# Head norms whose row transfers go by GpSimd's queue, in a hybrid attention, retention and pooling encoder

## The chip, the core and the metric

The kernel runs on one core of a Trainium2 chip. Five engines work side by side, each through its own instructions in a fixed order: TensorE (PE; its weight loads are shown as PEld), VectorE (DVE), ScalarE (ACT), GpSimd (POOL) and SyncE (SP), which here issues transfers. The metric is the device time of one execution in microseconds (us); lower is better.

## The reference

Two layers over a sequence of 512 tokens with 1024 features, then a final RMSNorm. Each layer normalises its input, projects it, gives the columns to three groups of heads, multiplies each group by its own SiLU gate and maps the three back with one output projection. The change concerns the norms at the end of the heads of groups A and B:

```python
# A: differential attention, 4 heads, values of 128 columns
o = rmsnorm(o, subln_w) * (1.0 - lam_init)
o_a = o.reshape(B_, S_, A_V_COLS) * jax.nn.silu(ag)
# B: bidirectional retention, 4 heads, values of 128 columns
o = o * lax.rsqrt(jnp.mean(o * o, axis=-1, keepdims=True) + EPS)
o_b = o_b * jax.nn.silu(bg)
# C: multi-scale pooling; then
mixed = jnp.concatenate([o_a, o_b, o_c], axis=-1)
return x + jnp.einsum('bse,ed->bsd', mixed, w_out)
```

So each of 2 x 8 heads needs one number per token, the reciprocal root of the mean square over its 128 features.

## The kernel before

All matmuls are in fp32 split into a high and a low part, three products for each (`mm3`): one 128x512 product is three matmuls. Weights come from DRAM as 512 KB pieces into `wraw` (2 buffers), and ACT and DVE split each into `wh` and `wl` (5 buffers each). A projection (`proj_T`, `proj_tok`) adds up 24 matmuls in one of three PSUM banks called `pj`. A gate (`gate`) is such a projection, a tanh on ACT and one multiply on DVE; that multiply is the last reader of its `pj` bank and so frees it.

A head ends with a result of 128 features (partitions) by 512 tokens in the one PSUM bank `ov`, and `headnorm` follows:

- ACT copies `ov` into `hn`, tokens reordered; DVE multiplies `ov` by the gate into `og`. `hn` and `og` have one buffer each, so the next head's copy waits for this head's last multiply.
- PE transposes `hn` into `tp` (4 matmuls of 128 columns), ACT squares and sums each quarter into `st` (the tile `st4`), DVE adds EPS, and GpSimd raises to the power -0.5: 512 numbers, 128 partitions by 4.
- A transfer writes these to a DRAM tile `row` of 512 numbers (`row<-st`), and a second one reads the row back into all 128 partitions of `hn` (`hn<-row`, 256 KB). The second waits for the first to land. Both are issued by SP, whose queue also issues the weight pieces and the decay and bias tables (`wide`).
- DVE multiplies `og` by `hn`, called the last multiply below, and the head is split into `mB` or `mAC` for the output projection.

The pooling heads use `hn` too, with windows of `u` that GpSimd clears.

The order of the instructions is not written by hand. The program is recorded as operations with their dependences; `schedule` then plays it through with a duration for each operation from `cost` and a delay between engines from `LATENCY`, and always starts next, on the engine that is free first, the ready operation of the highest rank. The order that comes out is each engine's fixed order. A transfer on SP is counted by the lines below (times in ns): it ends 1100 plus its bytes at 360 per ns plus 908 after its start, later when others are under way.

```python
            if e == "SP":
                bus = max(bus, start + 1100) + op.time
                op.end = bus + 908
```

All instructions are emitted at one line (L1055 before, L1057 after), so the profile is read by the names of the tiles.

Of the kernel before, what the change touches and what calls it, by code (L numbers as in the profile page):

```python
# [15 lines left out]
P = 128  # L16
# [153 lines left out]
class Recorder:  # L170
# [9 lines left out]
    def add(self, name, engine, method, args, kw):  # L180
# [33 lines left out]
        for b in bases:  # L214
            b.left += 1
        op.bases, op.deps, op.users = bases, list(deps.values()), []
        op.time, op.hold = cost(engine, method, args, kw)
        self.ops.append(op)

# [103 lines left out]
def cost(engine, method, args, kw):  # L323

    out = args[0]
    n = out.idx.size if isinstance(out, View) else 0
    psum = any(isinstance(a, View) and a.base.space == "psum" for a in args)
    if engine == "PE":
        if method == "transpose":
            return 109, 109  # L330
        f32 = args[1].base.dt == F32 and not any(s[0] == "bitcast" for s in args[1].steps)
        if f32:
            return 2 * 110 + 4 * n * 0.417, 2 * 110 + 4 * n * 0.417
        t = max(107, n * 0.417) + 2.5
        return t, t
    if engine == "SP":
        nbytes = (out.p1 - out.p0) * n * 4 if isinstance(out, View) and out.base.space != "dram" else P * D * 4
        if isinstance(out, View) and out.base.space == "dram":
            nbytes = 16384
        return nbytes / 360.0, 475  # L340
    if engine == "DVE":
        if method == "tensor_tensor":
            t = 1.041 * n + 69
        elif method == "scalar_tensor_tensor":
            t = 1.041 * n + (130 if isinstance(args[2], View) else 69)
        elif method == "tensor_scalar":
            t = (1.17 if psum else 0.64) * n + 69
        elif method == "tensor_copy":
            t = (1.04 if psum else 0.521) * n + 68
        elif method == "reciprocal":  # L350
            t = 6.2 * n + 69
        elif method == "memset":
            t = 9
        else:
            t = 1.041 * max(n, 2) + 75
        return t, t
    if engine == "ACT":
        t = 0.833 * n + (52 if psum else 94)
        for k in ("bias", "scale"):
            t += 93 * isinstance(kw.get(k), View)  # L360
        t += 93 * ("accum_out" in kw)
        return t, t
    if method == "tensor_tensor" and kw["op"] == ALU.pow:
        return 300 + 164 * n, 300 + 164 * n
    if method == "tensor_tensor":
        return 60 + 2.2 * n, 60 + 2.2 * n
    return 60 + 1.3 * n, 60 + 1.3 * n


def record(ins: dict, out: bass.AP):  # L370
    nc = Recorder()
    x_d = ins["x"][0]

    def sb(tag, shape, bufs=1, dt=F32, name=None):
        return nc.tile("sb", tag, shape, bufs, dt)
# [102 lines left out]
    def transpose4(src):  # L478

        tp = tpp()  # L480
        for j in range(4):
            nc.tensor.transpose(tp[:, j * P:(j + 1) * P], src[:, j * P:(j + 1) * P], ident)
        return tp.rearrange("p (j c) -> p j c", j=4)
# [51 lines left out]
    def headnorm(ov, scale, g):  # L535

        o = sb("hn", [P, UW], 1)[:, 0:S]

        nc.scalar.copy(o.rearrange("p (j c) -> p j c", j=4), ov.rearrange("p (c j) -> p j c", j=4))
        og = sb("og", [P, S], 1)  # L540
        nc.vector.scalar_tensor_tensor(og, ov, scale, g, op0=ALU.mult, op1=ALU.mult)
        tv = transpose4(o)
        st = sb("st4", [P, 8], 2)
        for j in range(4):
            nc.scalar.activation(o[:, j * P:(j + 1) * P], tv[:, j, :], AF.Square, accum_out=st[:, j:j + 1])
        nc.vector.tensor_scalar(st[:, 0:4], st[:, 0:4], 1.0 / P, EPS, op0=ALU.mult, op1=ALU.add)
        nc.gpsimd.tensor_tensor(st[:, 4:8], st[:, 0:4], neghalf, op=ALU.pow)
        row = nc.tile("dram", "row", [S], 4, F32)
        nc.sync.dma_start(row.rearrange("(p j) -> p j", j=4), st[:, 4:8])
        rb = o  # L550
        nc.sync.dma_start(rb, row.partition_broadcast(P))
        nc.vector.tensor_tensor(og, og, rb, op=ALU.mult)
        return og

# [126 lines left out]
    class Layer:  # L681
# [155 lines left out]
        def b_head(self, h):  # L837
            dt_ = chunk_decay(4 * self.l + h)
            qk, qx, sx = self.qk["B", h // 2]
            hd = h % 2  # L840
            ov = ovp()
            for ch in range(2):
                cs = slice(256 * ch, 256 * ch + 256)
                lg = lgp()
                for j in range(2):
                    ms = slice((2 * ch + j) * P, (2 * ch + j + 1) * P)
                    js = slice(256 * j, 256 * j + 256)
                    nc.tensor.matmul(lg[:, js], qk[:, 2 + 2 * hd, ms], qk[:, hd, cs], start=True, stop=False)
                    nc.tensor.matmul(lg[:, js], qk[:, 3 + 2 * hd, ms], qk[:, hd, cs], start=False, stop=True)
                s = soft()  # L850
                nc.vector.scalar_tensor_tensor(s.rearrange("p (j c) -> p j c", j=2), lg.rearrange("p (j c) -> p j c", j=2), 0.125,
                                               dt_[:, :, ::-1], op0=ALU.mult, op1=ALU.mult)
                it = ttile([P, 2, S], F32R)
                split(it[:, 0, :], it[:, 1, :], s)
                for j in range(2):
                    m, js = 2 * ch + j, slice(256 * j, 256 * j + 256)
                    mm3(ov[:, cs], self.vh[:, m, h * P:(h + 1) * P], self.vl[:, m, h * P:(h + 1) * P],
                        it[:, 0, js], it[:, 1, js], j == 0, False)
                for x in range(2):
                    nc.tensor.matmul(ov[:, cs], sx[:, hd, x, 1 - ch, :], qx[:, hd, cs], start=False, stop=x == 1)  # L860
            self.to_mixed("B", h, headnorm(ov, 0.5, self.gates["bg", h]))
# [7 lines left out]
        def a_head(self, h):  # L869
            qk = self.qk["A", h]  # L870
            bt = toeplitz(gdram, h)
            ov = ovp()
            for half in range(2):
                ah, al = ttile([P, NT, 256], F32R), ttile([P, NT, 256], F32R)
                for i2 in range(2):
                    i = half * 2 + i2
                    st = sb("sm", [P, 8], 4)
                    e = []
                    for mp in range(2):
                        lg = lgp()  # L880
                        mm_stacked(lg, qk, mp, slice(i * P, (i + 1) * P))
                        s = soft()

                        nc.vector.tensor_tensor_reduce(s, lg, toep_tile(bt, i), scale=1.0, scalar=3e38,
                                                       op0=ALU.add, op1=ALU.min, accum_out=st[:, mp:mp + 1])
                        nc.scalar.activation(s, s, AF.Exp, bias=st[:, mp:mp + 1], scale=-1.0, accum_out=st[:, 4 + mp:5 + mp])
                        e.append(s)
                    nc.vector.reciprocal(st[:, 6:8], st[:, 4:6])
                    nc.vector.tensor_tensor(st[:, 7:8], st[:, 7:8], lam_t[self.l], op=ALU.mult)
                    nc.scalar.activation(e[1], e[1], AF.Copy, scale=st[:, 7:8])  # L890
                    nc.vector.scalar_tensor_tensor(e[0], e[0], st[:, 6:7], e[1], op0=ALU.mult, op1=ALU.subtract)
                    tv = transpose4(e[0])
                    split(ah[:, :, i2 * P:(i2 + 1) * P], al[:, :, i2 * P:(i2 + 1) * P], tv)
                for kt in range(NT):
                    mm3(ov[:, half * 256:(half + 1) * 256], self.vh[:, kt, h * P:(h + 1) * P],
                        self.vl[:, kt, h * P:(h + 1) * P], ah[:, kt, :], al[:, kt, :], kt == 0, kt == NT - 1)
            self.og[h] = headnorm(ov, cols[:, self.l:self.l + 1], self.gates["ag", h])
# [225 lines left out]
```

## Time and profile before

| | us |
|---|---|
| Median of 3 runs (670.14 to 670.65) | 670.25 |
| Profiled execution, its own time | 670.98 |
| Its span, first to last instruction | 669.2 |
| PE busy | 657.1 |
| DVE busy | 478.3 |
| ACT busy | 385.2 |
| POOL busy | 30.2 |

A busy PE is not yet a PE at its peak: matmuls overlap, and one of 512 columns shows some 0.4 us while the next starts about 0.23 us after it. A pause of PE is therefore read from the starts of two neighbours. In brackets behind an instruction stands how long its engine was idle before it and what ended that.

### The profile page before, as it was taken

The page shows a single profiled execution, that of the slowest core. Times are in us where ns is not written, and L with a number is a line of the kernel's source. Part 1 is how long each engine was busy: PE and PEld are TensorE (multiplying, and loading weights), DVE is VectorE, ACT ScalarE, POOL GpSimd, SP SyncE. Part 2 cuts the span into 40 slices and gives each one's busy share as a digit, 9 for nine tenths or more (in the row PEclk, how much of TensorE's full clock was granted, in tenths as well). Part 3 has the DMA queues.
Part 4 walks back from the last instruction along what each step waited for, and adds up shares of the span by engine and source line. Part 5 has one row for each costly group of instructions (what it writes and reads, how often), then busy time and mean ns, then how long its engine had stood idle before and what let it go on. Part 6 is the DMA issues. An engine that isn't in the chain of part 4 may idle for free. (4 is left out here: it accounts for less than half of the span.)

```text
span 669.2 us, 8859 instructions
## 1 busy us (share of the span) xinstructions
PE 657.1 (98%) x3173; PEld 538.0 (80%) x3173; DVE 478.3 (71%) x865; ACT 385.2 (58%) x735; POOL 30.2 (5%) x51
## 2 busy tenths in 40 slices
PE   8999999999999999999999999999999999999996
PEld 6887878887788888887888788778888878888885
DVE  5798886776788879875754878587558846887733
ACT  6646885534776776552524877244567756874321
POOL 0100000000000000001010000000100000000011
PEclk9999999999999999999999999999999999999999
DMA  8545454223234322244113414433331243212302
GB/s 309 202 153 165 116 153 111 95 97 103 66 102 122 116 80 63 91 114 123 64 64 111 141 64 96 121 121 84 80 111 59 69 134 109 92 63 81 110 31 95
DMA packets 29300, 71.59 MB, mean 107 GB/s; under 512 B 5460, under 2 KB 9716, under 8 KB 29256
## 3 DMA queue, kind: packets, MB, share of 16 engines
q1 hardware_dynamic: 29256, 71.02, 34.4%
q8 instruction: 25, 0.41, 0.3%
q14 instruction: 19, 0.16, 0.1%
HBM read 68.83 MB, written 2.18 MB: 106 GB/s over the span
## 5 line engine op out<-in xcount | busy, mean ns | idle before, releaser
L1055 PE MATMUL pj<-hh,wh 128*128 128x512 f32 x448 | 176.9, 398 | 2.1 <-DVE gate L1055 1.3
L1055 PE MATMUL pj<-hl,wh 128*128 128x512 f32 x448 | 176.4, 395 | 0.0
L1055 PE MATMUL pj<-hh,wl 128*128 128x512 f32 x448 | 176.0, 396 | 0.0
L1055 ACT CAST wh<-wraw 128x1024 fp32r<-128x1024 f32 (+1 forms) x97 | 100.8, 1039 | 84.3 <-PE pj L1055 65.5
L1055 DVE TENSOR_TENSOR wl<-wraw,wh 128x1024 fp32r<-128x1024 f32 (+1 forms) x97 | 117.3, 1209 | 35.0 <-ACT wh L1055 34.5
L1055 PEld LDWEIGHTS pj<-hh,wh 128*128 128x128 f32 x448 | 84.1, 188 | 21.8 <-DVE gate L1055 1.9
L1055 PEld LDWEIGHTS pj<-hh,wl 128*128 128x128 f32 x448 | 84.0, 188 | 18.3
L1055 PEld LDWEIGHTS pj<-hl,wh 128*128 128x128 f32 x448 | 84.2, 188 | 17.8
L1055 PE MATMUL pj<-wh,mAC 128*128 128x512 f32 (+1 forms) x264 | 86.8, 390 | 0.0
L1055 ACT ACTIVATE soft<-soft,sm 128x512 f32<-128x512 f32 x96 | 68.6, 721 | 21.8 <-DVE sm L1055 20.8
L1055 DVE TENSOR_TENSOR x<-x,pj 128x512 f32<-128x512 f32 (+1 forms) x65 | 43.8, 676 | 19.7 <-PE pj L1055 19.2
L1055 PEld LDWEIGHTS pj<-wh,mAC 128*128 128x128 f32 x264 | 48.8, 188 | 10.3 <-DVE mAC L1055 0.2
L1055 PE MATMUL pj<-wl,mAC 128*128 128x512 f32 (+1 forms) x132 | 51.5, 390 | 0.0
L1055 PE MATMUL lg<-qk 128*128 128x512 f32 (+1 forms) x192 | 50.3, 360 | 0.7 <-DVE soft L1055 0.4
L1055 DVE CUSTOM_DVE_ANT_0 soft<-lg,wide 128x512 f32<-128x512 f32 x64 | 43.1, 686 | 9.7 <-PE lg L1055 7.0
L1055 POOL TENSOR_TENSOR st<-st,neghalf 128x4 f32<-128x4 f32 (+1 forms) x28 | 25.0, 892 | 476.2 <-DVE st L1055 447.5
L1055 PE MATMUL pj<-wh,mB 128*128 128x512 f32 (+1 forms) x136 | 44.3, 382 | 0.0
L1055 PE MATMUL pj<-wh,hh 128*128 128x512 f32 x104 | 41.3, 397 | 0.4 <-DVE vl L1055 0.4
L1055 PE MATMUL pj<-wl,hh 128*128 128x512 f32 x104 | 41.4, 398 | 0.0
L1055 PE MATMUL pj<-wh,hl 128*128 128x512 f32 x104 | 41.1, 396 | 0.0
L1055 PEld LDWEIGHTS lg<-qk 128*128 128x128 f32 x192 | 32.5, 188 | 8.0 <-issue 1.5
L1055 PE MATMUL ov<-T,vh 128*128 128x256 f32 x192 | 38.8, 283 | 0.0
(156 smaller groups left out, 951.6 us busy)
## 6 DMA issues: line engine op xcount, KB each, us to landing
wraw<-in_wg SPq DMA_DIRECT2D x95, 512.0 KB, 3.3
hn<-row SPq DMA_DIRECT2D x16, 256.0 KB, 3.4
wide<-gd SPq DMA_DIRECT2D x8, 448.0 KB, 3.1
T<-in_xT_w SPq DMA_DIRECT2D x8, 258.0 KB, 4.9
x<-in_x SPq DMA_DIRECT2D x8, 256.0 KB, 5.2
wide<-dd SPq DMA_DIRECT2D x8, 256.0 KB, 5.1
out<-T SPq DMA_DIRECT2D x8, 256.0 KB, 2.1
qd<-dd SPq DMA_DIRECT2D x8, 128.0 KB, 4.5
```

The source lines that it names most:

```text
L1055: op.inst = getattr(getattr(tc.nc, name), method)(*[real(a) for a in op.args], **{k: real(v) for k, v in op.kw.items()})
```

## The change

`headnorm` issues its two transfers through GpSimd's queue in place of SP's, and `cost` gets a row for transfers on GpSimd: 2000 ns to the end of one that writes DRAM, 3800 ns of any other, and 600 ns for which GpSimd is held by it.

```diff
+    if engine == "POOL" and method == "dma_start":
+        return (2000 if out.base.space == "dram" else 3800), 600
     if engine == "SP":
...
         nc.gpsimd.tensor_tensor(st[:, 4:8], st[:, 0:4], neghalf, op=ALU.pow)
         row = nc.tile("dram", "row", [S], 4, F32)
-        nc.sync.dma_start(row.rearrange("(p j) -> p j", j=4), st[:, 4:8])
+        nc.gpsimd.dma_start(row.rearrange("(p j) -> p j", j=4), st[:, 4:8])
         rb = o
-        nc.sync.dma_start(rb, row.partition_broadcast(P))
+        nc.gpsimd.dma_start(rb, row.partition_broadcast(P))
         nc.vector.tensor_tensor(og, og, rb, op=ALU.mult)
```

SP's list loses 32 transfers (189 rows become 157) and is otherwise in the same order; GpSimd's gets them, each pair right behind its power. Since the planner now counts other times, its order changes on the other engines as well. On PE the two orders are the same up to row 816 of 2850, differ in places up to about row 1145 and again from about row 1805 to about row 2340, and are the same elsewhere but for one matmul near the end.

First place: DVE in the second layer, around the last multiply of the first retention head (`og_3768`) and the gate multiply that frees bank `pj_3652`. Before:

```order
L1055 TENSOR_TENSOR T_3859<-soft_3847,T_3859 128x512
L1055 TENSOR_TENSOR og_3768<-og_3768,hn_3742 128x512
L1055 TENSOR_TENSOR T_3867<-soft_3856,T_3867 128x512
L1055 TENSOR_TENSOR qx_3841<-soft_3582,qx_3841 64x512
L1055 TENSOR_TENSOR mB_3885<-og_3768,mB_3885 128x512
L1055 SCALAR_TENSOR_TENSOR soft_3897<-lg_3861,wide_3869 128x512
L1055 SCALAR_TENSOR_TENSOR soft_3904<-lg_3872,wide_3869 128x512
L1055 TENSOR_TENSOR wl_3911<-wraw_3772,wh_3899 128x1024
L1055 TENSOR_TENSOR T_3908<-soft_3897,T_3908 128x512
L1055 SCALAR_TENSOR_TENSOR gate_3852<-gate_3852,pj_3652 128x512
```

The same place in the changed kernel:

```order
L1057 TENSOR_TENSOR T_3859<-soft_3847,T_3859 128x512
L1057 TENSOR_TENSOR T_3867<-soft_3856,T_3867 128x512
L1057 TENSOR_TENSOR og_3768<-og_3768,hn_3742 128x512
L1057 TENSOR_TENSOR qx_3841<-soft_3582,qx_3841 64x512
L1057 SCALAR_TENSOR_TENSOR gate_3852<-gate_3852,pj_3652 128x512
L1057 TENSOR_TENSOR mB_3889<-og_3768,mB_3889 128x512
```

The last multiply stands one instruction later, and the gate multiply two behind it where it stood eight behind it.

Second place: PE where the next projection takes the bank that this gate multiply frees (`pj_0`: the number after the tile's name is the buffer here). Before:

```order
L1055 MATMUL pj_2_3648<-hh_0_3084,wl_3_3478 128x512
L1055 MATMUL pj_2_3648<-hh_0_3084,wh_1_3459 128x512
L1055 MATMUL pj_0_3931<-hh_0_3084,wh_0_3640 128x512
L1055 MATMUL pj_0_3931<-hl_0_3094,wh_0_3640 128x512
L1055 MATMUL pj_0_3931<-hh_0_3084,wl_0_3655 128x512
```

In the changed kernel:

```order
L1057 MATMUL pj_1_3818<-hh_0_3084,wl_1_3619 128x512
L1057 MATMUL pj_2_3648<-hl_0_3094,wh_1_3459 128x512
L1057 MATMUL pj_0_3901<-hh_0_3084,wh_0_3640 128x512
L1057 MATMUL pj_0_3901<-hl_0_3094,wh_0_3640 128x512
L1057 MATMUL pj_0_3901<-hh_0_3084,wl_0_3655 128x512
```

The projection into bank `pj_0` begins at row 1806 in place of row 1824: behind the first of the 18 matmuls of `pj_2_3648` that all stood ahead of it before.

Third place: PE at the transposes of the second attention head of the second layer (`tp<-ident,hn`). Before:

```order
L1055 MATMUL pj_4894<-hh_3084,wl_4776 128x512
L1055 MATMUL tp_4959<-ident_219,hn_4953 128x128 x4
L1055 MATMUL pj_4894<-hh_3084,wh_4759 128x512
L1055 MATMUL pj_4894<-hl_3094,wh_4759 128x512
L1055 MATMUL pj_4894<-hh_3084,wl_4776 128x512
L1055 MATMUL pj_4970<-hh_3084,wh_4768 128x512
```

In the changed kernel:

```order
L1057 MATMUL pj_4895<-hl_3094,wh_4761 128x512
L1057 MATMUL pj_4895<-hh_3084,wl_4783 128x512
L1057 MATMUL pj_4964<-hh_3084,wh_4774 128x512
L1057 MATMUL tp_4966<-ident_219,hn_4958 128x128 x4
L1057 MATMUL pj_4964<-hl_3094,wh_4774 128x512
L1057 MATMUL pj_4964<-hh_3084,wl_4793 128x512
```

The transposes stand four matmuls of 512 columns later in the run of projections; those of the head before it stand one later (row 2279 in place of 2280, with eight matmuls of its projection left in place of nine).

## Rows read from the trace of the kernel before

**Rows 1.** The page's first part: busy us (share of the span) xinstructions.

```profile
PE 657.1 (98%) x3173; PEld 538.0 (80%) x3173; DVE 478.3 (71%) x865; ACT 385.2 (58%) x735; POOL 30.2 (5%) x51
```

**Rows 2.** Three stretches: from:to, length, busy PE, PEld, DVE, ACT, POOL, PE's clock.

```profile
191.00:270.00 79.00, 79.00 (x393) 65.29 (x392) 66.24 (x138) 56.61 (x114) 2.01 (x2) 1.00 0.34 105
270.00:423.00 153.00, 151.91 (x750) 124.89 (x749) 104.56 (x161) 83.79 (x154) 7.21 (x9) 1.00 0.33 97
423.00:555.00 132.00, 129.59 (x623) 106.01 (x622) 88.13 (x158) 72.26 (x151) 5.33 (x9) 1.00 0.31 92
```

**Rows 3.** Waits of PE: waiter <- waited for: us, times, longest.

```profile
PE pj L1055 <- DVE gate L1055: 1.3, 1, 1.3
PE tp L1055 <- ACT hn L1055: 1.2, 3, 0.7
```

**Rows 4.** Timeline of PE at its two longest pauses: start, length, instruction.

```profile
422.86 0.39 PE L1055 MATMUL pj<-hl,wh 128*128 128x512 f32 x1
...
426.82 0.40 PE L1055 MATMUL pj<-hh,wh 128*128 128x512 f32 x1
428.54 0.50 PE L1055 MATMUL pj<-hh,wh 128*128 128x512 f32 x1 [1.32 <-DVE gate L1055]
...
548.56 0.40 PE L1055 MATMUL pj<-hh,wl 128*128 128x512 f32 x1
549.63 0.33 PE L1055 MATMUL tp<-ident,hn 128*128 128x128 f32 x1 [0.67 <-ACT hn L1055]
```

**Rows 5.** Timeline of DVE ahead of the first pause.

```profile
419.81 0.69 DVE L1055 TENSOR_TENSOR T<-soft,T 128x512 fp32r<-128x512 f32 x1
422.23 0.69 DVE L1055 TENSOR_TENSOR og<-og,hn 128x512 f32<-128x512 f32 x1 [1.73 <-DMA hn<-row]
...
427.80 0.68 DVE L1055 SCALAR_TENSOR_TENSOR gate<-gate,pj 128x512 f32<-128x512 f32 x1
```

**Rows 6.** Timeline of POOL: three of the sixteen powers.

```profile
88.61 1.39 POOL L1055 TENSOR_TENSOR st<-st,neghalf 128x4 f32<-128x4 f32 x1 [35.81 <-DVE st L1055]
...
412.80 1.02 POOL L1055 TENSOR_TENSOR st<-st,neghalf 128x4 f32<-128x4 f32 x1 [28.67 <-issue]
...
622.30 1.01 POOL L1055 TENSOR_TENSOR st<-st,neghalf 128x4 f32<-128x4 f32 x1 [10.91 <-DVE st L1055]
```

**Rows 7.** Timeline of SP's queue (SPq) around the power at 412.80.

```profile
411.46 0.33 SPq L1055 DMA_DIRECT2D wraw<-in_wg  x1
413.29 0.38 SPq L1055 DMA_DIRECT2D wide<-dd  x1
413.84 0.33 SPq L1055 DMA_DIRECT2D row<-st  x1
417.98 0.32 SPq L1055 DMA_DIRECT2D hn<-row  x1
```

**Rows 8.** Timeline of DVE and ACT: four other last multiplies, and a copy behind one.

```profile
96.65 0.69 DVE L1055 TENSOR_TENSOR og<-og,hn 128x512 f32<-128x512 f32 x1 [0.21 <-DMA hn<-row]
...
478.56 0.69 DVE L1055 TENSOR_TENSOR og<-og,hn 128x512 f32<-128x512 f32 x1 [5.33 <-DMA hn<-row]
...
548.13 0.69 DVE L1055 TENSOR_TENSOR og<-og,hn 128x512 f32<-128x512 f32 x1 [3.48 <-DMA hn<-row]
548.99 0.59 ACT L1055 COPY hn<-ov 128x512 f32<-128x512 f32 x1 [6.14 <-DVE og L1055]
...
629.27 0.69 DVE L1055 TENSOR_TENSOR og<-og,hn 128x512 f32<-128x512 f32 x1 [0.82 <-DMA hn<-row]
```

**Rows 9.** Waits of DVE and of SP's queue for head norms: us, times, longest.

```profile
DVE og L1055 <- DMA hn<-row: 17.8, 9, 5.3
SPq L1055 <- POOL st L1055: 50.1, 16, 7.7
```

**Rows 10.** Transfers that touch `row` (both kinds), then `hn`: us from issue to landing.

```profile
DMA to landing us min/median/max: 1.4/3.4/4.7
...
DMA to landing us min/median/max: 3.2/3.4/4.7
```

## The prediction

> **What bounds the kernel now.** I read the page's first part first: PE is busy 657.1 us, 98% of the span of 669.2, DVE 71% and POOL 5% [rows 1]. So a gain can only come out of PE's pauses. The table by stretch shows where they lie, all at a granted clock of 1.00, the 2.4 GHz level. I carried the changed places of PE's order over to the trace by counting its matmuls: the first (row 817) is where the trace stands at 191 us, that part ends near 268, the second begins near 423 (row 1807 began at 422.86) and ends near 550. The first changed stretch has no pause at all (79.00 busy of 79.00), the second has 2.41 us, and the unchanged one between them 1.09 [rows 2].
>
> Then the waits: two pauses of the second stretch hang on head norms, one on a gate multiply and one on ACT's copy into `hn` [rows 3]. From the starts of neighbouring matmuls, less the usual 0.23, the first is 428.54 - 426.82 - 0.23 = 1.49 us, the second 549.63 - 548.56 - 0.23 = 0.84 [rows 4]. Together 2.33 us is what head norms visibly cost PE. DVE waits much longer for them, 17.8 us in nine waits [rows 9], but most of it reaches no one: its longest, 5.33 us [rows 8], has no pause of PE behind it.
>
> Why does DVE wait? Its order is the planner's, and on SP the planner counts the two transfers at 130 + 1100 + 45 + 908 and 1100 + 728 + 908 + 130 ns, 5.05 us from the end of the power to the last multiply. In the nine cases where DVE did wait, the trace has 6.65 for the first (88.61 + 1.39 = 90.00 to 96.65), 5.96 for the last (623.31 to 629.27) [rows 6, 8] and 8.41 for the longest (413.82 to 422.23) [rows 5, 6]; the mean of the nine is 6.54. The plan is 1.5 us short, and DVE, which takes its instructions in order, stands still for it.
>
> **The change part by part.**
>
> *The planner's numbers.* With 2.0, 3.8 and three times 0.06 us between the engines the plan now puts the last multiply 5.98 us behind the power, 0.93 later than before. That is where it stands, not how long it takes.
>
> *The chain on GpSimd.* No row shows a transfer from this queue. From below: the fastest row transfer and the fastest broadcast of SP, 1.4 + 3.2 = 4.6 us [rows 10]. From above: SP's longest chain, and for each transfer as much software as GpSimd's power needs (1.01 us [rows 6]): 8.41 + 2.02 = 10.4. Of these I take 6.0, near the last chain's 5.96, because SP's long chains are the ones that queued: at 413.84 the row transfer was issued behind a weight piece and a table, and the second could go only 4.14 us later [rows 7], where an undisturbed row lands in 1.4 [rows 10].
>
> The Trainium skill, DMA: Bandwidth & Descriptors, section Queues, rings and completion order, says that each transfer engine takes turns between the queues that have work for it. By that the 2 KB row would no longer stand behind 512 KB; no run here shows it yet, and with 1.4 + 3.4 the chain would be near 5.
>
> *First pause (428.54).* Before, the gate multiply stands eight instructions behind the last multiply and ends at 428.48 [rows 5]; PE wants the bank at 427.05. Now it stands two behind, but PE wants the bank 18 matmuls sooner, at 422.86 [rows 4]. On DVE five instructions of 0.69 then run from 419.81 on (T, T, the last multiply, qx, gate): ends at 423.25, PE at 423.30, a pause of 0.44. The last multiply is reached at 421.19, so any chain up to 7.3 us gives this. Gain 1.49 - 0.44 = 1.05. With the old 8.41 it would be: multiply at 422.23, gate done at 424.30, pause 1.49, no gain.
>
> *Second pause (549.63).* The head before has to finish its last multiply (548.13) before ACT may copy (548.99) [rows 8] and PE transpose. The transposes now stand four matmuls later, those of the head before one: 3 x 0.23 = 0.69 of the 0.84 is gone by order alone, the rest with a chain under 6.5 us. Gain 0.84.
>
> *SP's queue.* It no longer stands 50.1 us in front of head norms [rows 9], so weight pieces can start earlier. I count nothing: neither of the two pauses waited for a piece, and five buffers of `wh` lie ahead of PE. If that cover were gone it would show as waits of ACT for `wraw`.
>
> *GpSimd.* It is held for its two issues and for the row's landing. Queued behind are the next head's power and the clearing of `u`; at 5% busy [rows 1], with 10.91 to 35.81 us idle before the powers [rows 6], nobody waits for that.
>
> *What moves along.* 211 us of PE's order are dealt anew. Between: no fresh pause, as 191 to 270 has none now, and the density of the unchanged stretch, 1.09 in 153, on 211 us: 1.5 [rows 2]. I take the middle, 0.7.
>
> Sum: -1.05 - 0.84 + 0.7 = -1.2 us in the span of 669.2 [rows 1]; the 1.8 around it up to the profiled execution's 670.98 I leave as they are, so 669.8. The median of the runs was 0.73 below that execution; for the median 669.05.
>
> **The rivals.**
>
> B, the change doesn't do what it says, the new queue buys nothing: chains as on SP. The first place still waits as with 8.41 (gain 0), the second keeps 0.84 - 0.69 = 0.15 (gain 0.69), fresh pauses take 0.7: 670.25. For it: the same bytes go to the same memory. Against: the queueing at 413.84.
>
> C, slower: GpSimd's software lengthens both transfers, and DVE waits at all sixteen last multiplies, with gates, weight splits and mask multiplies queued behind. Price: today 17.8 us of DVE's waiting cost PE 2.33, or 0.13 for each. A chain of c us costs 16 x (c - 5.98) x 0.13. With fresh pauses it loses from c = 6.8 on; at 6.54 + 2 x 1.01 = 8.6 it is 5.5 - 2.33 + 0.7 = +3.9, so 674.1; at 10.4 about +7.6, 677.9. For it: GpSimd is the slowest engine in these rows, 1.01 us for four columns. Against: DVE's long wait of 5.33 cost nothing.
>
> The Trainium skill speaks for C: the same page, section Latency and other measured facts, gives about 1 us to the first byte from GpSimd's queue against 0.6 from SP's. As an estimate from that page two transfers make the mean 6.54 + 0.8 = 7.3, and by the price above +1.1, 671.4; no row here bears on it.
>
> D, the new order itself: a fresh pause of 3 us or so, like the two it removes together (2.33) and more, in the 211 us: 670.25 - 1.89 + 3.5 = 671.9. For it: the planner was 1.5 us off in one duration and may be in others. Against: 191 to 270 ran without one.
>
> **How the numbers follow.** About 0.2% (1.34 us) is what a measurement can tell from no change. The forecast, 0.60, is 669.05 with a range of its own from 667.3 (both pauses gone whole, nothing fresh, and a little from SP) to 670.7 (the fresh ones at 1.5 and half the gain); 0.32 of it lies under 668.91, 0.27 within, 0.01 above. B 0.19: 0.02, 0.16, 0.01. C 0.13: 0, 0.01, 0.12. D 0.08: 0, 0.02, 0.06. Faster 0.34, same 0.46, slower 0.20. The range goes to 667.2 below and, taking in D and the mild end of C, to 671.9 above.
>
> **What would show it.** Right: from the end of a power to the last multiply that waits, 5.5 to 6.5 us; DVE's wait for `hn` well under 17.8; no pause of PE over 0.6 for a gate near 423 and none over 0.3 for ACT's copy near 549; PE's pauses between 423 and 555 under 2.41 in sum. Wrong: chains over 7 us with longer waits of DVE (C), DVE's waits as before (B), or a pause of PE over 1 us that no head norm ends (D).

## The result: 674.74 us, slower by 0.57%, and the profile after

| | before | changed kernel |
|---|---|---|
| median of six runs | 670.58 us | 674.74 us (674.35 to 675.72) |
| ratio | 1 | 1.0057 [1.0040, 1.0073] |
| profiled execution, its span | 670.98, 669.2 us | 674.63, 672.8 us |
| DVE's wait for the broadcast row, sum | 17.8 us, nine times | 21.1 us, twelve times |
| chain from the power's end to the last multiply, mean where DVE waited | 6.54 us | 7.41 us (7.45 at the nine places of before) |

The forecast was 669.05 us with a range up to 671.9. The kernel became slower, by a way that stood among the rivals at 0.13.

The page's first part of the changed kernel (busy us, share of the span, instructions) answers to [rows 1]:

```profile
PE 658.2 (98%) x3173; PEld 538.3 (80%) x3173; DVE 477.9 (71%) x865; ACT 385.0 (57%) x735; POOL 48.9 (7%) x83
```

POOL has 32 instructions more, the issues. PE does the same 3173 matmuls; the span is longer by 3.6 us. The table by stretch (from:to, length, busy PE, PEld, DVE, ACT, POOL, PE's clock) answers to [rows 2]:

```profile
191.00:270.00 79.00, 77.67 (x385) 63.76 (x384) 66.21 (x136) 56.68 (x113) 4.33 (x6) 1.00 0.30 100
270.00:423.00 153.00, 152.20 (x754) 125.38 (x753) 105.78 (x165) 85.03 (x155) 10.69 (x15) 1.00 0.33 98
423.00:555.00 132.00, 128.48 (x616) 104.57 (x615) 85.72 (x154) 70.06 (x142) 8.96 (x16) 1.00 0.30 94
```

The first stretch, which had no pause, now lacks 1.33 us, the third 3.52 in place of 2.41; the middle one lost nothing (0.80 in place of 1.09). So most of the time is lost where the order was dealt anew; experiment 2 will show whether the order is to blame. From the starts of neighbouring matmuls, PE's gaps beyond the usual spacing sum to 3.6 us more than before over the whole span: that is what the span grew by. PE's own waits (us, times, longest), to be held against [rows 3]:

```profile
PE pj L1057 <- DVE gate L1057: 2.7, 1, 2.7
PE lg L1057 <- DVE sm L1057: 1.3, 2, 0.9
PE tp L1057 <- ACT hn L1057: 0.8, 3, 0.3
```

The gate multiply's pause doubled, the transposes' shrank, and a new one stands on a `sm` of DVE. In PE's timeline at the two forecast places ([rows 4] before):

```profile
424.76 0.40 PE L1057 MATMUL pj<-hl,wh 128*128 128x512 f32 x1
427.87 0.50 PE L1057 MATMUL pj<-hh,wh 128*128 128x512 f32 x1 [2.71 <-DVE gate L1057]
...
553.42 0.40 PE L1057 MATMUL pj<-hh,wh 128*128 128x512 f32 x1
554.12 0.66 PE L1057 MATMUL tp<-ident,hn 128*128 128x128 f32 x4 [0.30 <-ACT hn L1057]
```

427.87 - 424.76 - 0.23 = 2.88 us (was 1.49), and 554.12 - 553.42 - 0.23 = 0.47 (was 0.84). DVE's timeline, at the new pause's place and ahead of the first ([rows 5] before):

```profile
191.64 0.69 DVE L1057 TENSOR_TENSOR og<-og,hn 128x512 f32<-128x512 f32 x1 [1.58 <-DMA hn<-row]
192.25 0.68 DVE L1057 CUSTOM_DVE_ANT_0 soft<-lg,wide 128x512 f32<-128x512 f32 x1
192.86 0.08 DVE L1057 DVE_READ_ACCUMULATOR2_ANT sm<- 128x1 f32 x1
...
421.69 1.29 DVE L1057 TENSOR_TENSOR T<-soft,T 128x512 fp32r<-128x512 f32 x2
425.70 0.69 DVE L1057 TENSOR_TENSOR og<-og,hn 128x512 f32<-128x512 f32 x1 [2.72 <-DMA hn<-row]
426.42 0.69 DVE L1057 TENSOR_TENSOR qx<-soft,qx 64x512 fp32r<-64x512 f32 x1
427.12 0.69 DVE L1057 SCALAR_TENSOR_TENSOR gate<-gate,pj 128x512 f32<-128x512 f32 x1
```

The new pause is a head norm's too: the `sm` that PE waits for near 193 stands behind a last multiply that waited 1.58 us. At the first place the order is the one forecast: two `T`, the last multiply, `qx`, gate, nothing between. But the multiply, which DVE reached at 422.98, waits 2.72 us. POOL's timeline of that chain ([rows 6, 7] before):

```profile
414.65 1.02 POOL L1057 TENSOR_TENSOR st<-st,neghalf 128x4 f32<-128x4 f32 x1 [28.60 <-DVE st L1057]
416.08 0.61 POOL L1057 DMA_DIRECT2D row<-st  x1 [0.40 <-POOL st L1057]
420.20 0.54 POOL L1057 DMA_DIRECT2D hn<-row  x1 [3.52 <-DMA row<-st]
```

Power's end 415.67, multiply 425.70: a chain of 10.03 us where SP's had 8.41. Three parts make it. GpSimd begins its issue 0.41 us behind its own power (SP: 0.02). From there to the broadcast's issue it takes 4.12 us, as SP's 4.14, although the queue is its own. From the broadcast's issue to the multiply it takes 5.50, against 4.25. What SP did meanwhile is in its queue's timeline:

```profile
413.37 0.33 SPq L1057 DMA_DIRECT2D wraw<-in_wg  x1
415.19 0.38 SPq L1057 DMA_DIRECT2D wide<-dd  x1
419.10 0.33 SPq L1057 DMA_DIRECT2D wraw<-in_wg  x1
```

Before, SP issued the next weight piece behind the broadcast; now it issues it at 419.10, 1.10 us ahead of it. That piece alone does not explain the 1.25 us: in experiment 1 it goes 1.45 us ahead of the broadcast (420.16 and 421.61) and the same step takes 3.98 us, in experiment 8 it goes 0.28 us behind (417.20 and 416.92) and the step takes 4.88. Where the 1.25 us come from stays open. The trace's waits for the whole kernel ([rows 9] before):

```profile
POOL hn L1057 <- DMA row<-st: 35.0, 15, 3.5
DVE og L1057 <- DMA hn<-row: 21.1, 12, 4.1
ACT wh L1057 <- DMA wraw<-in_wg: 13.1, 12, 3.1
POOL row L1057 <- POOL st L1057: 6.1, 16, 0.4
```

GpSimd waits 0.38 us behind each of its sixteen powers (6.1) and 35.0 us for the row. And the transfers themselves, by tile: issue times in ns (min/median/max), then landing of both in us ([rows 10] before):

```profile
L1057 POOL DMA_DIRECT2D row<-st x16: 595/605/744, 90.1 to 627.4; - x16
L1057 POOL DMA_DIRECT2D hn<-row x16: 536/536/559, 93.4 to 629.8; - x16
...
DMA to landing us min/median/max: 1.7/3.4/5.5
```

SP's issues took 0.33 us each [rows 7]. On the quietest heads the row's issue stands 2.38 us ahead of the broadcast's, where SP had 1.42.

### The profile page after: what moved, and what is told of

It is laid out like the page before. It is cut to its first block, busy times and chain, and to the rows that moved or that the text cites. A ratio compares the mean times of both kernels' runs of the same rounds, so it can differ in the third digit from the quotient of the medians.

```text
span 672.8 us, 8859 instructions
## 1 busy us (share of the span) xinstructions
PE 658.2 (98%) x3173; PEld 538.3 (80%) x3173; DVE 477.9 (71%) x865; ACT 385.0 (57%) x735; POOL 48.9 (7%) x83
## 4 chain that ended last, share of the span: by engine, by line
PE 77%; DMA 9%; issue 4%; ACT 4%; DVE 4%; POOL 2%; POOLq 0%; ACTq 0%; DVEq 0%
PE pj L1057 61%; PE lg L1057 6%; PE ov L1057 5%; DMA hn<-row 5%; PE tp L1057 4%; DMA row<-st 3%; POOL st L1057 1%; ACT soft L1057 1%; DVE soft L1057 1%; ACT hn L1057 1%; DVE wl L1057 1%; DMA wide<-dd 1%; ACT wh L1057 1%; DVE og L1057 1%; ACT qk L1057 0%
## 5 line engine op out<-in xcount | busy, mean ns | idle before, releaser
L1057 PEld LDWEIGHTS pj<-hl,wh 128*128 128x128 f32 x448 | 84.2, 188 | 17.9
L1057 PEld LDWEIGHTS pj<-wh,mAC 128*128 128x128 f32 x264 | 48.9, 188 | 11.1 <-DVE mAC L1057 0.7
```

Of the source, the lines that this page charges most:

```text
L1057: op.inst = getattr(getattr(tc.nc, name), method)(*[real(a) for a in op.args], **{k: real(v) for k, v in op.kw.items()})
```

## The experiments

Times are ratios to the kernel before on the same chip, with 95% intervals; "wait" is DVE's for the broadcast row in the profiled execution. T1 (in the texts: theory 1) says that GpSimd's longer chains cost the time and the new order is innocent or a small gain; T2 that the new order itself costs, and the queue little.

**1. The queue alone.** The planner still sees SP; only the 32 issues change engine, so every engine keeps the order of before.

```diff
         nc.sync.dma_start(row.rearrange("(p j) -> p j", j=4), st[:, 4:8])
+        nc.ops[-1].method = ("gpsimd", "dma_start")
         rb = o
         nc.sync.dma_start(rb, row.partition_broadcast(P))
+        nc.ops[-1].method = ("gpsimd", "dma_start")
```

> The kernel before with its order on every engine kept word for word; only the 32 row transfers are issued by GpSimd instead of SP. Theory 1 (the chain): from GpSimd the chain from the power to the last multiply is some 0.8 us longer (7.3 against 6.5 on average), DVE stands still for it and PE after DVE; the order is innocent. It expects chains of 7.3, DVE's wait for hn at 30 us or more (17.8 before, 0.8 more at each of 9 to 16 places), and 2 to 3 us slower than before (ratio 1.003 to 1.0045). Theory 2 (the order): the new order, in which the users stand closer behind, costs the time, whatever the queue. It expects this run within 0.1% of before (670.0 to 671.2).

Measured: 1.0178 [1.0154, 1.0203], median 683.55; the profiled execution took 678.38, 7.4 us more than before's. Wait 27.7 us, twelve times. At the nine places where DVE had waited before, the chain is 0.67 us longer in the mean. PE's worst place, in its timeline and DVE's:

```profile
190.14 0.40 PE L1057 MATMUL pj<-wh,hl 128*128 128x512 f32 x1
192.55 0.66 PE L1057 MATMUL tp<-ident,soft 128*128 128x128 f32 x4 [2.02 <-DVE soft L1057]
```

```profile
187.81 0.16 DVE L1057 TENSOR_TENSOR sm<-sm,cols 128x1 f32<-128x1 f32 x1
191.14 0.69 DVE L1057 TENSOR_TENSOR og<-og,hn 128x512 f32<-128x512 f32 x1 [3.18 <-DMA hn<-row]
191.75 0.74 DVE L1057 SCALAR_TENSOR_TENSOR soft<-soft,sm,soft 128x512 f32<-128x512 f32 x1
```

PE does not wait for the head norm; it waits for a `soft` that merely stands behind the last multiply on DVE. So a wait list of PE that names `soft` or `sm` can hide a head norm. T2 falls. T1 has the direction right and the size 4 to 6 times too small by the runs, about 3 times by the profiled execution (7.4 us for 2 to 3); part of the difference between the two is the clock of experiment 11. The wait, 27.7, stayed under the 30 or more that it named.

**2. The order alone.** The changed kernel's plan, the transfers issued by SP.

```diff
         nc.gpsimd.dma_start(row.rearrange("(p j) -> p j", j=4), st[:, 4:8])
+        nc.ops[-1].method = ("sync", "dma_start")
         rb = o
         nc.gpsimd.dma_start(rb, row.partition_broadcast(P))
+        nc.ops[-1].method = ("sync", "dma_start")
```

> The changed kernel with its order on every engine kept, but the 32 transfers issued by SP again. Theory 1 (the chain): chains are back at 6.5 against the 6.0 that this order was planned for, DVE's wait for hn falls under 17.8, and the time is 0 to 1.3 us under before (ratio 0.998 to 1.000). Theory 2 (the order): as slow as the changed kernel, ratio 1.005 to 1.006, with the pause of PE near 425 of 2 us or more still there.

Measured: 0.9958 [0.9943, 0.9973]; profiled 668.95, wait 11.1 us, six times. Its first place:

```profile
421.22 0.69 DVE L1059 TENSOR_TENSOR og<-og,hn 128x512 f32<-128x512 f32 x1 [1.14 <-DMA hn<-row]
...
421.89 0.40 PE L1059 MATMUL pj<-hl,wh 128*128 128x512 f32 x1
423.39 0.50 PE L1059 MATMUL pj<-hh,wh 128*128 128x512 f32 x1 [1.10 <-DVE gate L1059]
```

The same instructions in the same order as in the changed kernel pause PE for 1.27 us there (423.39 - 421.89 - 0.23), not 2.88, and the chain is 8.40 (from the power's end at 412.82), not 10.03. The order is good and the queue bad: the two parts of the change have opposite signs. The gain is larger than T1's range, 0.998 to 1.000.

**3, 4. Count the chain longer.** If the plan is what matters, a plan that expects more must win on either queue. On GpSimd (planned chain 7.38 us in place of 5.98):

```diff
-        return (2000 if out.base.space == "dram" else 3800), 600
+        return (3000 if out.base.space == "dram" else 4200), 600
```

> The changed kernel, transfers on GpSimd's queue, but the planner counts them 3000 and 4200 ns, 7.4 us for the chain, as the changed kernel's trace shows on average. Theory 1 (the chain against its plan): DVE's wait for hn falls to under 12 us (21.1 in the changed kernel), the pauses that followed late multiplies go, ratio to before 0.998 to 1.002. Theory 2 (the order): a third order, with fresh pauses of its own; nothing makes it better than the second, ratio 1.003 to 1.006.

Measured: 0.9921 [0.9901, 0.9941]; wait 9.4, four times. On SP, from the kernel before (planned 5.05 + 1.5):

```diff
-                op.end = bus + 908
+                op.end = bus + 908 + op.late    # late = 750 for the row and its broadcast, else 0
```

> The kernel before, transfers on SP, but the planner counts each of the 32 transfers 750 ns longer, 6.55 us for the chain, as the trace of before shows on average. Theory 1 (the chain against its plan): chains stay 6.5, DVE's wait for hn falls from 17.8 to under 8 us, and the two pauses of PE at head norms (2.33 us) go: 0.7 to 2 us faster, ratio 0.997 to 0.999. Theory 2 (the order): a new order brings its own pauses as the changed kernel's did, ratio 1.000 to 1.004.

Measured: 0.9932 [0.9912, 0.9951]; wait 6.4, three times. Both gains are larger than T1's ranges, which began at 0.998 and 0.997. GpSimd's chains did not get shorter in experiment 3 (10.06 at the first place, where DVE's wait is 1.37 us in place of 2.72). DVE has other work in front of the multiply.

**5. That longer plan, issued by SP.** Experiment 3's line and both of experiment 2.

```diff
-        return (2000 if out.base.space == "dram" else 3800), 600
+        return (3000 if out.base.space == "dram" else 4200), 600
...
+        nc.ops[-1].method = ("sync", "dma_start")
```

> The order of the run that counted 3000 and 4200 ns, kept on every engine, but the 32 transfers issued by SP. Theory 1 (the chain against its plan): the order has room for 7.4 us, so the shorter chains of SP gain little: within 0.2% of the same order on GpSimd (ratio to before 0.990 to 0.994), DVE's wait for hn under 9.4 us. A rival, the queue itself (GpSimd's transfers free SP for the weight pieces and so make this order fast): back to 0.996 or more, with longer waits of ACT for wraw.

Measured: 0.9902 [0.9881, 0.9923], median 665.97: the lowest ratio of all, faster than both kernels. Its DVE timeline at the first place, and its third stretch:

```profile
418.82 0.69 DVE L1059 TENSOR_TENSOR qx<-soft,qx 64x512 fp32r<-64x512 f32 x1
419.52 0.69 DVE L1059 SCALAR_TENSOR_TENSOR gate<-gate,pj 128x512 f32<-128x512 f32 x1
420.14 0.69 DVE L1059 TENSOR_TENSOR og<-og,hn 128x512 f32<-128x512 f32 x1
```

```profile
423.00:555.00 132.00, 132.00 (x637) 108.63 (x636) 89.21 (x158) 74.26 (x153) 5.32 (x9) 1.00 0.30 96
```

Gate multiply and `qx` now stand ahead of the last multiply, which no longer waits (the 8.56 us of its chain are covered), and PE is busy in the whole of the third stretch, where the changed kernel lacks 3.52 us.

**6, 7. Longer still.** Is there a price for counting too much? SP's, from experiment 4, and GpSimd's, from experiment 3:

```diff
-        nc.ops[-1].late = 750
+        nc.ops[-1].late = 1250
...
-        return (3000 if out.base.space == "dram" else 4200), 600
+        return (3600 if out.base.space == "dram" else 4800), 600
```

> The kernel before, on SP, each of the 32 transfers counted 1250 ns longer (7.55 us for the chain, where 750 made 6.55). Theory 1: chains of SP are 5.5 to 8.8, so the waits left over go too: ratio 0.990 to 0.994, DVE's wait for hn under 6 us. Rival (each order has pauses of its own by chance): anywhere from 0.992 to 1.002.

> Transfers on GpSimd counted 3600 and 4800 ns, 8.6 us for the chain, 1.2 more than the mean of what they take. Theory 1: little is left to gain, and the single buffers of hn and og are held longer by the plan: ratio 0.990 to 0.995. Rival (chance of the order): 0.992 to 1.004.

Measured: 0.9911 [0.9890, 0.9932] and 0.9915 [0.9893, 0.9936]. Another 1 or 1.2 us in the plan changes nothing that can be told apart. Between 0.9902 and 0.9932 the five runs of long plans have intervals that overlap: no difference between the queues can be told any more once the plan has room. That four different orders all gain speaks against chance; both rivals began at 0.992, just above the 0.9911 and 0.9915 measured, though within their intervals.

**8. What the row stands behind.** The changed kernel, but the second layer's decay table (256 KB, read from DRAM in shifted runs of 1 KB) is replaced by a read of a constant in runs of 2 KB, so that layer's decays are left out.

```diff
-        nc.sync.dma_start(t, ddram.window(row, 256, [[1, P], [P, 2], [1, 256]]))
+        nc.sync.dma_start(t, (ddram.window(row, 256, [[1, P], [P, 2], [1, 256]]) if row < 4
+                              else ins["c_cos"].rearrange("p (j c) -> p j c", j=2)))
```

> The changed kernel, order unchanged, with one source changed: in the second layer the 256 KB decay table is read from a constant in runs of 2 KB instead of from its own DRAM tile in shifted runs of 1 KB (so the decays of that layer are left out). At the first pause the row transfer needed 4.1 us, issued behind a weight piece and this table, on either queue. If the row stands behind the table's slow runs on the transfer engines: row to second issue there 2.4 to 3.0 us, chain 10.0 down to 8 or less, pause of PE 2.9 down to 1.2 or less, 1 to 2 us faster than the changed kernel (ratio to before 1.002 to 1.005). If it is only the amount of bytes in flight, or GpSimd's software: chain and pause as in the changed kernel, ratio 1.005 to 1.007.

Measured: 0.9992 [0.9972, 1.0012]; profiled 669.96, 4.7 us under the changed kernel's. GpSimd's issues and PE at the first place:

```profile
414.18 0.61 POOL L1057 DMA_DIRECT2D row<-st  x1 [0.41 <-POOL st L1057]
416.92 0.54 POOL L1057 DMA_DIRECT2D hn<-row  x1 [2.13 <-DMA row<-st]
```

```profile
422.85 0.40 PE L1057 MATMUL pj<-hl,wh 128*128 128x512 f32 x1
423.97 0.50 PE L1057 MATMUL pj<-hh,wh 128*128 128x512 f32 x1 [0.72 <-DVE gate L1057]
```

From the row's issue to the broadcast's 2.74 us in place of 4.12, the chain 8.03 in place of 10.03, the pause 0.89 in place of 2.88. The 2 KB row did wait for the table's transfer, from a queue of its own too. What in the table holds it is not shown: the table's own runs also overlap in one row of 4 KB and begin at another offset for each partition, and the run length, the overlap and the source changed together. The gain in time is more than was expected: counted by PE's matmuls, 3.9 of the 4.7 us lie between 405 and 555 us, after that layer's tables are read, and 2.0 of these are this pause.

**9, 10. Each transfer alone.** The order of before; only the row, or only the broadcast, goes by GpSimd. The row's edit (the broadcast's is the same line behind its own transfer):

```diff
         nc.sync.dma_start(row.rearrange("(p j) -> p j", j=4), st[:, 4:8])
+        nc.ops[-1].method = ("gpsimd", "dma_start")
         rb = o
         nc.sync.dma_start(rb, row.partition_broadcast(P))
```

> The order of before on every engine; only the 2 KB row transfer is issued by GpSimd, the broadcast by SP. Read from the traces so far GpSimd's part is 0.38 instead of 0.03 us from the power to the issue and 2.4 instead of 1.4 from issue to the next issue in a quiet place, and about nothing in the broadcast. By that reading the row carries most of the cost: chains some 0.6 longer, ratio 1.008 to 1.018. If it is the broadcast (128 runs of 2 KB made by software), this run stands near before, 1.000 to 1.004.

> The order of before on every engine; the 2 KB row transfer by SP, only the broadcast by GpSimd. By the reading that the row carries the cost: chains within 0.2 of before, ratio 0.999 to 1.005. If the broadcast does: 1.008 to 1.018.

Measured: 1.0064 [1.0036, 1.0092] and 1.0064 [1.0042, 1.0085]. Each alone costs about a third of both together. My reading that the row carries the cost is wrong by the traces too: at the nine places where DVE waited before, the chain is 0.31 us longer with the row alone and 0.32 with the broadcast alone, against 0.67 with both (0.95 in experiment 11's profile of the same kernel). Each part is seen at its shortest: from the power's end to the broadcast's issue 1.44 us with both on SP, 2.08 with the row alone, 1.95 with the broadcast alone, 2.55 with both on GpSimd. So, as far as single profiles tell, the two share the cost about evenly. That in time two halves make less than the whole fits a plan whose slack is used up by the first half, but was not tested.

**11, 12. What the profiled execution did not show.** Experiment 1's timed runs lie 4 to 7 us above its profiled one, at a mean granted clock of 0.992 to 0.996 in place of 0.999. Experiment 10's profiled execution (681.27 us, 0.993) had two stretches at the lower level, near 226 and 438 us, behind pauses of PE of 2.62 and 2.63 us. Experiment 1's kernel and the changed one once more, unchanged.

> The kernel of e1 once more (order of before on every engine, the 32 transfers issued by GpSimd), for a second profiled execution: e1's profiled one took 678.38 us at a mean granted clock of 0.999, its timed runs 682.4 to 685.0 at 0.992 to 0.996. Theory K (the clock): the timed runs lose about 5 us because PE's granted clock falls to its lower level (1.2 GHz) for some 3 us behind a pause of 2 us or more that a last multiply leaves; an execution of 682 or more then shows matmuls of 512 columns spaced 0.43 us in place of 0.23 right behind such a pause, about 1.4 us lost at each, and a mean clock of 0.996 or less. Theory L (more waiting): at 682 or more the clock stays at 0.998 or above, and PE's pauses sum to 4 us more than in e1's profile (DVE's wait for hn 32 us or more in place of 27.7). An execution near 678 with a clock of 0.999 tells nothing.

> The changed kernel once more, for a second profiled execution: its first took 674.63 us at 0.999, others 674.35 to 675.72 at 0.995 to 0.997. Theory K: at a mean clock of 0.996 or less there is a stretch at the lower level behind a pause of PE of 2 us or more (the 2.88 us pause for the gate near 424.9 first of all), with 1 to 1.5 us lost in it. Theory L: no such stretch. DVE's wait for hn 20 to 23 us and the pause near 424.9 of 2.4 to 3.2 us under both.

Measured: 687.18 us at a clock of 0.991 and 677.12 at 0.996. In the second, PE's timeline behind the gate's pause, and two of the next stretches:

```profile
426.19 0.40 PE L1057 MATMUL pj<-hl,wh 128*128 128x512 f32 x1
429.06 0.50 PE L1057 MATMUL pj<-hh,wh 128*128 128x512 f32 x1 [2.47 <-DVE gate L1057]
...
430.09 0.39 PE L1057 MATMUL pj<-hl,wh 128*128 128x512 f32 x1
430.32 0.55 PE L1057 MATMUL pj<-hh,wl 128*128 128x512 f32 x1
...
431.09 0.63 PE L1057 MATMUL pj<-hl,wh 128*128 128x512 f32 x1
431.52 0.63 PE L1057 MATMUL pj<-hh,wl 128*128 128x512 f32 x1
```

```profile
430.00:431.00 1.00, 1.00 (x5) 0.81 (x4) 1.00 (x3) 0.62 (x1) 0.00 (x0) 0.70 0.00 0
431.00:432.00 1.00, 1.00 (x4) 0.71 (x3) 1.00 (x2) 0.00 (x0) 0.00 (x0) 0.50 0.12 47
```

Behind a pause of 2.64 us the granted clock falls to 0.50, the 1.2 GHz level: the spacing goes from 0.23 to 0.43 us until 433.97, nine matmuls in 3.65 us that would take 2.10, so 1.55 lost. The other execution shows two such stretches, from 194.4 to 197.9 behind a pause of 2.36 (about 1.6 lost) and from 437.5 to 443.6 behind one of 2.95 (2.8 lost). Together 4.4 of its 8.8 us beyond experiment 1's profile. The rest is more waiting: DVE's is 31.6 us in place of 27.7, and the pauses of PE are longer. So for that kernel the clock that K names is about half of the 8.8 us and the added waiting that L names the other half, although L's own sign, a clock of 0.998 or above, did not come. In the changed kernel the clock is 1.55 of 2.5 us. The fall is not certain: in the first profile of the changed kernel the pause of 2.88 left the clock at 1.00.

## Why the prediction was wrong, point by point

**What bounds the kernel: right.** The time followed PE's pauses: 3.6 us more of them, 3.6 us more span.

**The order: right in direction, too small.** The two moves and the fresh pauses were worth -1.2 us in the sum. The order alone was worth 2.0 us of profiled time (0.42% in the runs). Only 0.75 of that stands at the two pauses (1.49 to 1.27, 0.84 to 0.31), and 0.8 lies between 288 and 405 us, where PE's order did not change; so what the working had named is only a part of the gain. With SP's chain of 8.40 at the first place the pause was 1.27 us; the working had 1.49 for 8.41. No fresh pause of PE near 3 us came while the chain stayed SP's, so rival D falls.

**The chain on GpSimd: the step that failed.** "Of these I take 6.0" measured 7.41 in the mean where DVE waited, inside the bounds 4.6 to 10.4, and no chain of the changed kernel was under 6.5. This term accounts for the whole miss: with the same order and SP's transfers the profiled execution took 668.95 us (experiment 2), where the forecast had 669.8. I took the value of SP's last chain, because I put SP's long chains down to queueing on SP. The rows could have told me that I had nothing for that: the last chain, 5.96, had no GpSimd issue in it. What the 6.0 left out is 0.35 us more between the power and the issue, 0.2 to 0.3 more for each issue, and the rest on the way to the landing; on quiet heads the step from the row's issue to the broadcast's has grown by about 1 us (1.42 to 2.38).

Two places of the Trainium skill stood beside that step. The Trainium skill, DMA: Bandwidth & Descriptors, section Latency and other measured facts, gives about 1 us to the first byte from GpSimd's queue against 0.6 from SP's. As an estimate from that page of the Trainium skill the chain was 7.3, and the trace agrees in the sum, with 7.41. The Trainium skill, DMA: Bandwidth & Descriptors, section Queues, rings and completion order, says that each transfer engine takes turns between the queues. From that I had concluded that the row would not stand behind the loads; here it did, since it took 4.12 us from a queue of its own and 4.14 from SP's. What shortened it was another source and form of the table (experiment 8).

**The first pause: the condition failed.** "Any chain up to 7.3 us gives this", a pause of 0.44; the chain was 10.03 and the pause 2.88. The working behind it holds: the gate multiply ends 2.1 us behind the last multiply's start, and PE begins right after. The new order is not what lost here: the order of before, with a chain of 10.17 us at this place (experiment 11), pauses PE for the same gate by 437.49 - 434.31 - 0.23 = 2.95 us:

```profile
434.31 0.40 PE L1057 MATMUL pj<-hh,wh 128*128 128x512 f32 x1
437.49 0.79 PE L1057 MATMUL pj<-hh,wh 128*128 128x512 f32 x1 [2.77 <-DVE gate L1057]
```

In either order a chain of 8.4 us left a pause of 1.27 to 1.49, and one of 10.0 to 10.2 a pause of 2.88 to 2.95: it is the chain that sets this pause.

**The second pause: right for the order, half right for the size.** 0.84 was to go whole; 0.47 is left with a chain of 7.44, where the gain was tied to one under 6.5. With SP's transfers 0.31 was left, by a chain of 7.29.

**Rival C's price: the other term that was mis-sized.** C named the mechanism (longer transfers by GpSimd, DVE waits at more multiplies with other work behind). But it took 2.33 / 17.8 = 0.13 us of PE for each us of DVE's wait, an average over waits that the old plan's slack had covered. With the same order, 10.0 us more wait (21.1 against 11.1) cost 674.63 - 668.95 = 5.7 us, 0.57 for each. With the order of before, 9.9 us more (27.7 against 17.8) cost 7.4, 0.75 for each. With the chain at 7.41 C's price gave 16 x 1.43 x 0.13 - 1.63 = +1.3 us; 4 were measured. So the mean price was four to six times too low for the added microseconds. It also counted only pauses whose wait names a head norm, and experiment 1's worst one names a `soft`. Nor is the new price a constant: in experiment 8 the wait fell by 3.2 us (21.1 to 17.9) and the time by 4.7, though the tables' other form may have helped elsewhere too.

**SP's queue and GpSimd: right.** SP's 50.1 us of standing went away. ACT's wait for weight pieces was 13.1 us in place of 16.1, but 15.6 in the changed kernel's second profile, so no fall is shown. Nor is a gain: experiments 3 and 5, one plan on either queue, differ by 0.2% in SP's favour, inside their intervals. The other engines' waits for GpSimd are as before.

**Rival B** falls as well: the chains were not as on SP.

Not settled: what makes the 1.25 us behind the broadcast's issue at the first place, and what in the table's form or source holds up the row. Not tried: the table loaded earlier into a second buffer.

## What to carry to other kernels

In a kernel whose order is planned, a small transfer's planned time has to be the whole chain as a trace shows it, from the producer's end to the consumer's start; here a plan that was 1.4 to 1.5 us short lost to every plan that was not, and counting 1 us too much cost nothing that could be measured. Each us of wait that the queue added cost 0.57 to 0.75 us. Change the queue and the plan one at a time: here the plan alone gave -0.42%, the queue alone +1.8%, and a longer plan -0.7 to -1.0% on either queue. Price a wait by what stands behind it on its engine, not by the average of waits that were covered.

## What the runs showed of the hardware that was not expected

- GpSimd's issue of a transfer took 0.54 to 0.61 us (the first one 0.74) against SP's 0.33, and began 0.29 to 0.41 us behind GpSimd's own result that it moves; SP began 0.03 behind the same result.
- A 2 KB transfer from a queue of its own was held up as long (4.12 us) as on the queue of the large loads (4.14). It took 2.74 us when the table was read from another source in runs of 2 KB in place of overlapping ones of 1 KB; which of these differences decides is not shown.
- Pauses of 2.36 to 2.95 us of PE were followed, in some executions and not in others, by 3 to 6 us at the 1.2 GHz level, 1.5 to 2.8 us lost each time in the three stretches worked out. Experiment 5's profile has no pause of PE over 0.6 us and no such stretch up to its last matmul, and its six executions stood at 0.997 to 0.999. The kernel before, whose profile has no pause over 1.49 us, also had executions at 0.995; those were not profiled, so what lowered their clock is not known.
